# Two more weight slots from a 1 KB descriptor space, and the recurrent gate's 1 - a^2 without a reciprocal

## The chip, the cores and the metric

The kernel runs on one core of a Trainium2 chip. The metric is the device time of one execution in microseconds, and the median of the runs counts. The engines named below are PE (TensorE, with PEld for its weight loads), DVE (VectorE), ACT (ScalarE), POOL (GpSimd) and SP (SyncE, which here does little but issue DMAs).

## The reference

Two transformer blocks run one after the other over 256 tokens of width 1024, batch 1, all in fp32. The first is a hybrid layer: sparse latent attention (each query keeps 64 keys by an index score) beside a gated recurrence. The second has two attentions and a mixture of 32 experts, of which each token takes two. The change touches the recurrence:

```python
r = sigmoid(xb @ w_a + b_a);  i = sigmoid(xb @ w_x + b_x)        # 16 blocks of 64 channels
log_a = -8 * r * softplus(-lam)
a = exp(log_a)
b_in = sqrt(-expm1(2 * log_a)) * (i * x)
h_t = a_t * h_(t-1) + b_in_t                                      # scan over 256 tokens
```

and the way in which all weights, those of the experts above all, come in:

```python
(silu(xb @ w_g[e]) * (xb @ w_u[e])) @ w_d[e]                      # 32 experts, 1024 -> 256 -> 1024
```

## The kernel before

**Weights.** They are one flat DRAM array, cut into pieces, most of them [128, 2048] fp32, that is 1 MB or 8 KB per partition. `load` issues one DMA per piece from SP's queue, in the order of the list `PIECES`: first the dense layers' pieces of both blocks, then per group q of four experts eight pieces gu{q}_0..7 (gate and up) and four pieces dn{q}_0..3 (down). A piece goes into a slot of 8 KB per partition of the pool `bigp`, which has `NBIG` = 19 of them (L26) and shares them with the large activations. `live` counts slots that activations hold; `piece(name)` lets the loads run ahead by what is left. In the expert stage the pieces rotate through `NBIG - 1 + NMO` = 22 slots, four of which are opened late.

**Dense layers.** For each weight piece `split` (L231 to L243) makes a high part (ACT copy, L241) and the rest (a subtraction, L242, on DVE, and on POOL for every second), and `mm3` (L251, L254) multiplies three times per 128 rows. Between pieces `tick()` takes one step from the list `todo`: the choice of 64 keys, the convolution `rnn_conv` (L590, L592), the gates `rnn_gate` (L596 to L611), the attention of a head pair (`attend`, L364 to L403), the scans `rnn_scan` (L613 to L619).

**The gate.** There are eight channel tiles of 128 channels. For tile m, PE makes the two gate products (pg, L600), ACT the tanh of both (L603), a = exp(...) into la (L605) and tt = tanh(u) with u = -log a (L606). Then 1 - a^2 = 2 tanh(u) / (1 + tanh(u)): DVE adds 1 (L607), takes the reciprocal (L608) and multiplies (L609) into `yy`; L610 makes the gated input `ix`. When all eight are there, one square root over 128x2048 elements on ACT (L616, which needs a table load of ACT before it, and another one after it for the next exp or tanh), eight POOL products (L617) and eight DVE scans (L618, printed as TENSOR_TENSOR_SCAN in the trace and as SCALAR_TENSOR_TENSOR in the written order) follow.

**Attention.** `attend` makes the logits of two heads on PE; DVE adds the mask and takes the extreme (L380), ACT makes the exp (L381), DVE the reciprocal of the sums (L382) and the scaling (L384); PE transposes (pt, L391), ACT copies (L393), PE multiplies with the values.

**Experts.** After the router (`trir`, L1021 to L1023, is a constant triangle and a block of ones that PE uses in L1122 to L1127 to rank tokens) each group of four experts gathers its tokens (px L1183, xe L1185), multiplies by gate and up (`products`, pgu L1219), builds the matrix that spreads its result (`spread`, GW L1202 on DVE, pw L1205 on PE), and runs the down product of the group before it (`outputs`: py L1246 on PE, ys L1249 on DVE, acc L1325 on PE, a quarter of the columns at a time). L1354 adds the residual in the round of group 5. L1367 reads a count of further rounds, `nri`, from SP's queue; the loop behind it runs zero times here.

**Order.** A scheduler that simulates a timeline writes the order of each engine's instructions when the kernel is built. Slots, pools and the length of an operation enter into it, so that the order can change at places that the code of the change doesn't touch.

Of the kernel before, what the change touches and what calls it, by code (L numbers as in the profile page):

```python
# [10 lines left out]
F32R = mybir.dt.float32r  # L11
I32 = mybir.dt.int32
AF = mybir.ActivationFunctionType
ALU = mybir.AluOpType
# [3 lines left out]
P = 128  # L18
T = 256
# [3 lines left out]
TAKEN = -3e38  # L23
SLOT = 32
FILL = -2e38
NBIG, NMO, NS2, SPARE, POOLDIV = 19, 4, 7, 0, 2  # L26
KW = 5
SLOPES = [2.0 ** (-0.5 * (h + 1)) for h in range(16)]

# [48 lines left out]
def tile_two_blocks(ctx: ExitStack, tc: tile.TileContext, w, xT_d, xtk_d, vecs_d, rows_d, consa_d, consb_d, wr_d, lam_d, out_d):  # L78
    nc = tc.nc

    cst = ctx.enter_context(tc.tile_pool(name="cst", bufs=1))
# [11 lines left out]
    def gone(n):  # L93

        live[0] -= n
# [8 lines left out]
    def big3(name, dt=F32, m=8):  # L104
        return big(name, dt).rearrange("p (m t) -> p m t", m=m)

    def s2(name, dt=F32, cols=512):
        return s2p.tile([P, cols], dt, tag="s2", name=name)
# [7 lines left out]
    def pst(name):  # L116
        return psp.tile([P, 512], F32, tag="t", name=name)
# [462 lines left out]
    la = big3("la")  # L580
    yy = big("yy")
    yy3 = yy.rearrange("p (m t) -> p m t", m=8)
# [11 lines left out]
    def rnn_gate(m):  # L594
        xc = xcs[m]
        pg = pst("pg")  # L596
        for g in range(2):
            for r0 in (0, 64):
                r = slice(r0, r0 + 64)
                nc.tensor.matmul(pg[r, g * T:(g + 1) * T], rgv[r, m, g, :], xc[r, :T], start=True, stop=True)  # L600
        rt = s2("rt")
        for g in range(2):
            nc.scalar.activation(rt[:, g * T:(g + 1) * T], pg[:, g * T:(g + 1) * T], AF.Tanh, bias=hb[:, 16 + 8 * g + m:17 + 8 * g + m], scale=0.5)  # L603
        tt = s2("tt")
        nc.scalar.activation(la[:, m, :], rt[:, 0:T], AF.Exp, bias=nsp4[:, m:m + 1], scale=nsp4[:, m:m + 1])  # L605
        nc.scalar.activation(tt[:, 0:T], rt[:, 0:T], AF.Tanh, bias=sp4[:, m:m + 1], scale=sp4[:, m:m + 1])  # L606
        nc.vector.tensor_scalar(tt[:, T:2 * T], tt[:, 0:T], 1.0, None, ALU.add)  # L607
        nc.vector.reciprocal(tt[:, T:2 * T], tt[:, T:2 * T])  # L608
        nc.vector.scalar_tensor_tensor(yy3[:, m, :], tt[:, 0:T], 2.0, tt[:, T:2 * T], ALU.mult, ALU.mult)  # L609
        nc.vector.scalar_tensor_tensor(ix[:, m, :], rt[:, T:2 * T], 1.0, xc[:, :T], ALU.add, ALU.mult)  # L610
        gone(m // 7)  # L611

# [13 lines left out]
    for m in range(8):  # L626
        st = [[L(pick, m)], [L(rnn_gate, m)]]
        if m < 7:
            st[0].append(L(rnn_conv, m + 1))
        if m < 4:  # L630
            st[1].append(L(head_k, m))
        elif m < 6:
            st[1].append(L(head_v, m - 4))
        todo += st
# [103 lines left out]
    for i in range(4):  # L738
        ps = mmp("p_wo")
        dense_fm(ps, f"wo{i}", at(mixh), at(mixl), late=i == 0)  # L740
        for j in range(2):
            m = 2 * i + j
# [4 lines left out]
        for j in range(2):  # L747
            m = 2 * i + j
# [31 lines left out]
    for i in range(4):  # L780
# [4 lines left out]
        for j in range(2):  # L785
            m = 2 * i + j
# [190 lines left out]
    def out2(which, i, j):  # L977
        ps = mmp("p_o" + which)
        o = obo[which]
        dense_fm(ps, f"o{which}{i}", at(o), at(o, 4), 4, 512, T * j)  # L980
        return ps, slice(4 * i + 2 * j, 4 * i + 2 * j + 2)

    tga = big3("tga")
    for i in range(2):
        gate2("g2a", 2 * i, tga)
        gate2("g2a", 2 * i + 1, tga)
        for j in range(2):
            ps, m = out2("a", i, j)
# [11 lines left out]
    for i in range(2):  # L1000
        for j in range(2):
            ps, m = out2("b", i, j)
# [15 lines left out]
    for t in (lg[:, :, 36:44], em[:, :, 32:40], top, gtop):  # L1018
        nc.gpsimd.memset(t, FILL)

    trir = cst.tile([P, 2, P], F32R, name="trir")  # L1021
    nc.gpsimd.tensor_copy(trir[:, 0, :], tri)
    nc.gpsimd.tensor_copy(trir[:, 1, :], ones)  # L1023
    ssx = cst.tile([P, 2, 4], F32, name="ssx")
# [493 lines left out]
```

## Time and profile before

| | |
|---|---|
| median of 3 runs | 723.87 us (723.16 to 725.01) |
| profiled execution, its own time | 725.25 us |
| its span | 723.1 us |
| PE busy | 677.8 us, 94% of the span |
| weight loads of PE | 558.9 us, 77% |
| DVE / ACT / POOL busy | 425.4 / 323.8 / 236.6 us |
| read from HBM | 176.67 MB |

A busy share is an average over a dense part, in which PE is nearly always busy, and an expert part from about 515 us on, in which the DMA queue is also busy without a break. The profile's end of a matmul is modelled, so a "busy" PE may be waiting inside. The count and the busy time of the weight loads (PEld) show better how fast a stretch goes forward. In the views, "idle before, releaser" is the time for which an engine sat idle before an instruction and what ended it.

### The profile page before, as it was taken

The numbers are of one execution on the slowest core, as the hardware profiler recorded it, in microseconds if no ns is written. First come the engines' busy times: TensorE is split into PE (matmuls) and PEld (weight loads), VectorE is DVE, ScalarE is ACT, GpSimd is POOL, SyncE is SP. The second block draws the span as 40 slices with busy tenths as digits, with TensorE's granted clock in tenths as the row PEclk, the third lists the DMA queues.
The fourth block names the chain that finished last, engine by engine and source line by source line (L and its number), as shares of the span: only waits on it lengthen the run. The fifth ranks groups of instructions, "written<-read, shape, count | busy, mean of one in ns | idle before, by whom it ended". The sixth has DMA issues, their size and how long they took to land. (4 is left out here: it accounts for less than half of the span.)

```text
span 723.1 us, 13963 instructions
## 1 busy us (share of the span) xinstructions
PE 677.8 (94%) x5463; PEld 558.9 (77%) x5463; DVE 425.4 (59%) x1043; ACT 323.8 (45%) x714; POOL 236.6 (33%) x194
## 2 busy tenths in 40 slices
PE   8989998979999999999999999999999999989983
PEld 7979887968999999998899989999645544534532
DVE  3977999897654767889645565275533222222224
ACT  6355587766755557656476466554100000001022
POOL 1344343466534656965332333372000000000002
PEclk8999999999999999999999999999999999999997
DMA  8991115324647537451035616587899999999992
GB/s 323 417 418 71 60 46 189 117 82 158 228 161 306 184 131 291 159 181 70 5 140 207 233 60 228 180 337 304 336 420 420 419 421 421 420 419 421 420 408 75
DMA packets 26855, 178.69 MB, mean 247 GB/s; under 512 B 3104, under 2 KB 4000, under 8 KB 6176
## 3 DMA queue, kind: packets, MB, share of 16 engines
q1 hardware_dynamic: 26352, 177.15, 62.8%
q8 instruction: 45, 0.74, 0.4%
q10 hardware_dynamic: 432, 0.59, 0.2%
q14 instruction: 26, 0.21, 0.1%
HBM read 176.67 MB, written 1.05 MB: 246 GB/s over the span
## 5 line engine op out<-in xcount | busy, mean ns | idle before, releaser
L1302 POOL TENSOR_TENSOR xg<-xo,fin 128x256 f32<-128x256 f32 (+1 forms) x10 | 6.0, 634 | 211.9 <-DMA w_dn<-in_w_dram 209.4
L1219 PE MATMUL pgu<-w_gu,xe 128*32 128x512 f32 x512 | 65.1, 598 | 0.4 <-DMA w_gu<-in_w_dram 0.4
L1224 ACT ACTIVATE th<-pgu,ss 128x256 f32<-128x256 f32 x8 | 3.8, 475 | 132.8 <-PE pgu L1219 132.8
L1249 DVE COPY ys<-py 128x256 f32<-128x256 f32 (+1 forms) x33 | 13.7, 416 | 46.9 <-PE py L1246 46.8
L1219 PEld LDWEIGHTS pgu<-w_gu,xe 128*32 128x32 f32 x512 | 14.7, 109 | 27.9 <-issue 24.9
L1183 PEld LDWEIGHTS px<-G,xT 128*128 128x128 f32 x256 | 30.2, 192 | 7.6 <-issue 5.5
L1185 DVE TENSOR_TENSOR xe<-px,vecs 128x256 f32<-128x256 f32 (+1 forms) x34 | 13.8, 409 | 37.3 <-PE px L1183 37.3
L1325 PE MATMUL acc<-ys,gwT 128*128 128x256 f32 x112 | 30.6, 405 | 3.5 <-DVE ys L1249 3.5
L1183 PE MATMUL px<-G,xT 128*128 128x128 f32 x256 | 31.9, 278 | 1.4 <-DVE G L1171 0.9
L251 PE MATMUL p_qkv<-hl,hh 128*128 128x256 f32 x192 | 33.2, 294 | 0.0
L381 ACT ACTIVATE lg<-lg,mx 128x128 f32<-128x128 f32 x64 | 28.3, 445 | 8.9 <-DVE mx L380 8.9
L1325 PEld LDWEIGHTS acc<-ys,gwT 128*128 128x128 f32 x112 | 19.6, 190 | 14.6 <-DVE ys L1249 6.6
L251 PEld LDWEIGHTS p_qkv<-hl,hh 128*128 128x128 f32 x192 | 27.7, 198 | 0.3 <-issue 0.2
L1225 DVE SCALAR_TENSOR_TENSOR th<-th,pgu 128x256 f32<-128x256 f32 x8 | 3.4, 421 | 36.8 <-ACT th L1224 36.8
L384 DVE TENSOR_SCALAR lg<-lg,sm 128x128 f32<-128x128 f32 x64 | 21.3, 376 | 0.9
L254 PE MATMUL p_qkv<-hl,hl__3332 128*128 128x256 f32 x96 | 20.3, 293 | 0.0
L391 PE MATMUL pt<-consa,lg 128*128 128x128 f32 x96 | 14.7, 279 | 4.4 <-DVE lg L384 4.4
L242 POOL TENSOR_TENSOR hl<-w_mr,hl 128x512 fp32r<-128x512 f32 x8 | 10.9, 1374 | 20.5 <-ACT hl L241 20.5
L242 POOL TENSOR_TENSOR hl<-w_g2a,hl 128x512 fp32r<-128x512 f32 x8 | 10.4, 1302 | 22.0 <-ACT hl L241 17.8
L251 PE MATMUL p_gr<-xh,hl 128*128 128x256 f32 x64 | 17.6, 302 | 0.0
L251 PE MATMUL p_w<-hl,m2h 128*128 128x256 f32 x96 | 16.2, 284 | 1.2 <-ACT m2h L359 1.2
L592 DVE SCALAR_TENSOR_TENSOR xc<-xr,vecs,xc 128x256 f32<-128x256 f32 x24 | 17.2, 715 | 0.1
(550 smaller groups left out, 2308.9 us busy)
## 6 DMA issues: line engine op xcount, KB each, us to landing
w_gu<-in_w_dram SPq DMA_DIRECT2D x64, 1024.0 KB, 19.8
w_dn<-in_w_dram SPq DMA_DIRECT2D x31, 1024.0 KB, 19.8
w_xr<-in_w_dram SPq DMA_DIRECT2D x4, 1024.0 KB, 11.2
w_q<-in_w_dram SPq DMA_DIRECT2D x4, 1024.0 KB, 17.0
w_mr<-in_w_dram SPq DMA_DIRECT2D x4, 1024.0 KB, 19.8
w_ma<-in_w_dram SPq DMA_DIRECT2D x4, 1024.0 KB, 5.1
w_gr<-in_w_dram SPq DMA_DIRECT2D x4, 1024.0 KB, 4.8
w_rp<-in_w_dram SPq DMA_DIRECT2D x4, 1024.0 KB, 5.1
```

The source lines that it names most:

```text
L242: e.tensor_tensor(l, view, h.bitcast(F32), ALU.subtract)
L251: nc.tensor.matmul(out, l_(k), r_(k), start=first and i == 0, stop=last and i == n - 1)
L254: nc.tensor.matmul(out, al(k), bh(k), start=first and i == 0, stop=last and i == n - 1)
L381: nc.scalar.activation(lg[:, c0:c1], lg[:, c0:c1], AF.Exp, bias=mx[:, b:b + 1], scale=-1.0, accum_out=sm[:, b:b + 1])
L384: nc.vector.tensor_scalar(lg[:, c0:c1], lg[:, c0:c1], sm[:, b:b + 1], None, ALU.mult)
L391: nc.tensor.transpose(pt[:, i * P:(i + 1) * P], pr[hd][:, i * P:(i + 1) * P], ident)
L592: nc.vector.scalar_tensor_tensor(xc[:, :T], xr[:, kk:kk + T], vec(V_CW, kk * 8 + m), xc[:, :T], ALU.mult, ALU.add)
L1183: nc.tensor.matmul(px[:, j * P:(j + 1) * P], x2[:, k, b, :], G[:, b], start=b == 0, stop=b == 1)
L1185: nc.vector.tensor_tensor(xg[k // 4][:, k % 4:k % 4 + n, :], v3(px, n, P), gain2(k, n), ALU.mult)
L1219: nc.tensor.matmul(pgu[32 * j:32 * j + 32, :], xg[k // 4][:, k % 4, 32 * j:32 * j + 32], wgu[:, 512 * j:512 * j + 512], start=k == 0, stop ...
L1249: nc.vector.tensor_copy(ys[:, :n], py[:, :n])
L1325: nc.tensor.matmul(acc[0][:, b, c // 512, c % 512:c % 512 + n], lhsT, rhs, start=q == 0 and c % 512 == 0, stop=q == 6 and c % 512 == T)
```

## The change

There are four edits. (1) `NBIG` goes from 19 to 21: two more slots of 8 KB per partition, and so 24 instead of 22 in the expert stage's rotation. (2) In the gate, 1 - a^2 is made as tanh(u) (1 + a^2): one product of la with itself, and one operation that adds 1 and multiplies by tanh(u); the addition and the reciprocal go. (3) `trir` has no place of its own among the constants any longer but takes one of the seven rotating 2 KB slots `s2`. (4) The program's dynamic DMA scratch size (a space for descriptors that is set aside in SBUF) is set to 1024 bytes.

```diff
--- before.py
+++ after.py
@@ -23,7 +23,7 @@
 TAKEN = -3e38
 SLOT = 32
 FILL = -2e38
-NBIG, NMO, NS2, SPARE, POOLDIV = 19, 4, 7, 0, 2
+NBIG, NMO, NS2, SPARE, POOLDIV = 21, 4, 7, 0, 2
 KW = 5
 SLOPES = [2.0 ** (-0.5 * (h + 1)) for h in range(16)]
 
@@ -604,9 +604,9 @@
         tt = s2("tt")
         nc.scalar.activation(la[:, m, :], rt[:, 0:T], AF.Exp, bias=nsp4[:, m:m + 1], scale=nsp4[:, m:m + 1])
         nc.scalar.activation(tt[:, 0:T], rt[:, 0:T], AF.Tanh, bias=sp4[:, m:m + 1], scale=sp4[:, m:m + 1])
-        nc.vector.tensor_scalar(tt[:, T:2 * T], tt[:, 0:T], 1.0, None, ALU.add)
-        nc.vector.reciprocal(tt[:, T:2 * T], tt[:, T:2 * T])
-        nc.vector.scalar_tensor_tensor(yy3[:, m, :], tt[:, 0:T], 2.0, tt[:, T:2 * T], ALU.mult, ALU.mult)
+
+        nc.vector.tensor_tensor(tt[:, T:2 * T], la[:, m, :], la[:, m, :], ALU.mult)
+        nc.vector.scalar_tensor_tensor(yy3[:, m, :], tt[:, T:2 * T], 1.0, tt[:, 0:T], ALU.add, ALU.mult)
         nc.vector.scalar_tensor_tensor(ix[:, m, :], rt[:, T:2 * T], 1.0, xc[:, :T], ALU.add, ALU.mult)
         gone(m // 7)
 
@@ -1018,7 +1018,7 @@
     for t in (lg[:, :, 36:44], em[:, :, 32:40], top, gtop):
         nc.gpsimd.memset(t, FILL)
 
-    trir = cst.tile([P, 2, P], F32R, name="trir")
+    trir = s2("trir", F32R, 2 * P).rearrange("p (b c) -> p b c", b=2)
     nc.gpsimd.tensor_copy(trir[:, 0, :], tri)
     nc.gpsimd.tensor_copy(trir[:, 1, :], ones)
     ssx = cst.tile([P, 2, 4], F32, name="ssx")
@@ -1504,7 +1504,7 @@
     from concourse import mybir as _mybir
     from concourse.bass_utils import run_bass_kernel_spmd as _run
 
-    nc = _bacc.Bacc("TRN2", target_bir_lowering=False, num_devices=1)
+    nc = _bacc.Bacc("TRN2", target_bir_lowering=False, num_devices=1, dynamic_dma_scratch_size=1024)
     arrays, args = {}, []
     for name, a in _pack(inputs):
         a = np.ascontiguousarray(a)
```

The written order moves at three places that matter for what follows. The first is ACT, around the square root of the gates. A name such as `w_gr_1260` is the 1 MB piece that is being split, `tma` a merge gate's tanh, `lg` the logits of a head. Before:

```order
L606 ACTIVATE tt<-rt,sp_427 128x256
L241 ACTIVATE hl<-w_gr_1260 128x512 x3
L678 ACTIVATE tma<-g,hb 128x256 x2
L381 ACTIVATE lg,sm<-lg,mx 128x128
L241 ACTIVATE hl<-w_gr_1260 128x512
L381 ACTIVATE lg,sm<-lg,mx 128x256
L616 ACT_TABLE_LOAD
L616 ACTIVATE yy<-yy 128x2048
L241 ACTIVATE hl<-w_gr_1471 128x512
L381 ACT_TABLE_LOAD
L381 ACTIVATE lg,sm<-lg,mx 128x128
```

and ACT at the same place of the changed program:

```order
L606 ACTIVATE tt<-rt,sp_431 128x256
L241 ACTIVATE hl<-w_gr_855 128x512
L616 ACT_TABLE_LOAD
L616 ACTIVATE yy<-yy 128x2048
L241 ACTIVATE hl<-w_gr_855 128x512
L678 ACT_TABLE_LOAD
L678 ACTIVATE tma<-g,hb 128x256 x2
L381 ACTIVATE lg,sm<-lg,mx 128x128
L241 ACTIVATE hl<-w_gr_855 128x512
L381 ACTIVATE lg,sm<-lg,mx 128x256
```

The root stood between the exps of the first head pair, with a table load on either side; now it stands ahead of all of them, behind the last gate and one weight copy. On DVE the scans that hang on the root stand behind the first pair's logits in both programs, but three of them now stand together ahead of the pair's softmax sums. Before:

```order
L382 RECIPROCAL sm<-sm 128x2
L384 TENSOR_SCALAR lg<-lg,sm 128x128
L384 TENSOR_SCALAR lg<-lg,sm 128x256
L380 ISA lg,mx<-ps_s,dm 128x128
L380 ISA mx 128x1
L380 ISA lg,mx<-ps_s,dm 128x256
L380 ISA mx 128x1
L242 TENSOR_TENSOR hl<-w_gr_1471,hl 128x512
L618 SCALAR_TENSOR_TENSOR ix<-la,yy 128x256
```

and DVE in the changed program:

```order
L380 ISA lg,mx<-ps_s,dm 128x256
L380 ISA mx 128x1
L618 SCALAR_TENSOR_TENSOR ix<-la,yy 128x256 x3
L242 TENSOR_TENSOR hl<-w_gr_855,hl 128x512
L382 RECIPROCAL sm<-sm 128x2
L380 ISA lg,mx<-ps_s,dm 128x128
L380 ISA mx 128x1
L380 ISA lg,mx<-ps_s,dm 128x256
L380 ISA mx 128x1
L618 SCALAR_TENSOR_TENSOR ix<-la,yy 128x256
L384 TENSOR_SCALAR lg<-lg,sm 128x128
```

Before, the first head's sums and scaling (L382, L384) stood ahead of the first scan; now they stand behind three of them. The second place is SP's queue where the router's count `nri` is read. Before:

```order
L130 DMA w_dn_0_6210<-in_w_dram 128x2048
L130 DMA w_gu_1_6359<-in_w_dram 128x2048
L130 DMA w_dn_3_6355<-in_w_dram 128x2048
L130 DMA w_dn_1_6351<-in_w_dram 128x2048
L130 DMA w_dn_2_6353<-in_w_dram 128x2048
L130 DMA w_gu_0_6357<-in_w_dram 128x2048
L1367 TENSOR_LOAD nri
L1367 ISA x2
```

and SP in the changed program:

```order
L130 DMA w_dn_0_6061<-in_w_dram 128x2048
L130 DMA w_dn_1_6142<-in_w_dram 128x2048
L130 DMA w_dn_2_6206<-in_w_dram 128x2048
L130 DMA w_gu_3_6355<-in_w_dram 128x2048
L130 DMA w_gu_1_6351<-in_w_dram 128x2048
L130 DMA w_dn_3_6347<-in_w_dram 128x2048
L130 DMA w_gu_0_6349<-in_w_dram 128x2048
L130 DMA w_gu_2_6353<-in_w_dram 128x2048
L1367 TENSOR_LOAD nri
L1367 ISA x2
```

Two more loads stand ahead of the read. The third place is PE in the expert stage, at the outputs of the fourth group (`py` its down products, `acc` the sum over groups, `pw` the spread matrix of the next group). Before:

```order
L1219 MATMUL pgu<-w_gu_7_6419,xe 32x512 x4
L1205 MATMUL pw<-consa,GW 128x128 x2
L1246 MATMUL py<-w_dn_0_6421,hT__7104 32x256 x8
L1325 MATMUL acc<-ys,gwT 128x256 x2
L1246 MATMUL py<-w_dn_1_6423,hT__7104 32x256 x8
L1246 MATMUL py<-w_dn_2_6425,hT__7104 32x256 x8
L1325 MATMUL acc<-ys,gwT 128x256 x2
L1246 MATMUL py<-w_dn_3_6427,hT__7104 32x256 x8
L1325 MATMUL acc<-ys,gwT 128x256 x4
L1354 MATMUL acc<-xT,consa 128x512 x4
```

and PE at the same place of the changed program:

```order
L1219 MATMUL pgu<-w_gu_7_6411,xe 32x512 x4
L1205 MATMUL pw<-consa,GW 128x128
L1246 MATMUL py<-w_dn_0_6413,hT__7096 32x256 x8
L1205 MATMUL pw<-consa,GW 128x128
L1246 MATMUL py<-w_dn_1_6415,hT__7096 32x256 x8
L1325 MATMUL acc<-ys,gwT 128x256 x4
L1246 MATMUL py<-w_dn_2_6417,hT__7096 32x256 x8
L1325 MATMUL acc<-ys,gwT 128x256 x2
L1246 MATMUL py<-w_dn_3_6419,hT__7096 32x256 x8
L1325 MATMUL acc<-ys,gwT 128x256 x2
L1354 MATMUL acc<-xT,consa 128x512 x4
```

A down product now stands between the two spread products, and the sums follow two down products instead of one. The two casts of `trir` on POOL moved from the program's start to behind the last weight split.

## Rows read from the trace of the kernel before

**Rows 1.** The page's parts on span and busy time (share, instructions).

```profile
span 723.1 us, 13963 instructions
PE 677.8 (94%) x5463; PEld 558.9 (77%) x5463; DVE 425.4 (59%) x1043; ACT 323.8 (45%) x714; POOL 236.6 (33%) x194
```

**Rows 2.** Windows: PE, PEld, DVE, ACT, POOL busy; granted clock; DMA share; GB/s.

```profile
96.00:108.00 12.00, 11.39 (x95) 10.29 (x91) 11.93 (x17) 9.97 (x22) 5.74 (x5) 1.00 0.17 53
108.00:120.00 12.00, 10.79 (x80) 9.08 (x79) 11.97 (x16) 10.16 (x22) 5.28 (x5) 1.00 0.60 213
120.00:132.00 12.00, 10.98 (x85) 9.16 (x85) 11.89 (x18) 7.91 (x17) 3.77 (x3) 1.00 0.50 177
144.00:156.00 12.00, 9.84 (x72) 7.91 (x70) 11.65 (x19) 7.82 (x22) 11.38 (x10) 1.00 0.00 0
156.00:168.00 12.00, 9.74 (x69) 8.70 (x67) 10.22 (x28) 8.06 (x21) 5.46 (x4) 0.86 0.72 260
180.00:192.00 12.00, 12.00 (x102) 11.09 (x101) 8.96 (x30) 8.86 (x24) 8.14 (x5) 1.00 0.75 264
```

**Rows 3.** PE's waits, 84 to 168 us: total, times, longest.

```profile
PE pt L391 <- DVE lg L384: 4.4, 4, 2.3
```

**Rows 4.** DVE by line, 84 to 144 us: busy, mean ns, idle before.

```profile
L608 DVE RECIPROCAL tt<-tt 128x256 f32<-128x256 f32 x8 | 14.0, 1751 | 0.2
L607 DVE TENSOR_SCALAR tt<-tt 128x256 f32<-128x256 f32 x8 | 2.8, 346 | 0.7 <-ACT tt L606 0.7
L609 DVE SCALAR_TENSOR_TENSOR yy<-tt 128x256 f32<-128x256 f32 x8 | 4.4, 552 | 0.0
L526 DVE TENSOR_TENSOR dm<-wk,consb 128x256 f32<-128x256 f32 x1 | 0.4, 415 | 0.0
```

**Rows 5.** The gate's tiles: ns min/median/max, first and last start.

```profile
L608 DVE RECIPROCAL tt<-tt x8: 1740/1754/1756, 88.6 to 135.2; 128x256 f32<-128x256 f32 x8
L609 DVE SCALAR_TENSOR_TENSOR yy<-tt x8: 411/414/1520, 90.8 to 138.6; 128x256 f32<-128x256 f32 x8
```

**Rows 6.** Timelines of ACT, POOL and DVE at the root: start, us.

```profile
139.90 1.28 ACT L616 ACT_TABLE_LOAD   x1
141.19 1.91 ACT L616 ACTIVATE yy<-yy 128x2048 f32<-128x2048 f32 x1
143.65 1.28 ACT L381 ACT_TABLE_LOAD   x1
...
143.18 7.26 POOL L617 TENSOR_TENSOR yy<-yy,ix 128x256 f32<-128x256 f32 x8 [2.40 <-ACT yy L616]
...
144.40 1.22 DVE L618 TENSOR_TENSOR_SCAN ix<-la,yy 128x256 f32<-128x256 f32 x1
```

**Rows 7.** SP's waits over the span, and the page's row of its queue.

```profile
SPq L130 <- DVE hl L242: 306.6, 46, 24.4
...
q1 hardware_dynamic: 26352, 177.15, 62.8%
```

**Rows 8.** Windows of the expert stage, columns as in Rows 2.

```profile
528.00:612.00 84.00, 79.92 (x678) 41.46 (x674) 23.88 (x76) 4.29 (x10) 0.00 (x0) 1.00 1.01 420
612.00:696.00 84.00, 76.92 (x594) 38.87 (x594) 20.62 (x67) 3.55 (x8) 0.00 (x0) 0.96 1.01 420
```

**Rows 9.** PE's waits, 600 to 712 us.

```profile
PE pgu L1219 <- DMA w_gu<-in_w_dram: 0.4, 1, 0.4
```

**Rows 10.** PE's timeline at the outputs of two groups: start, us.

```profile
609.08 0.33 PE L1205 MATMUL pw<-consa,GW 128*128 128x128 f32 x1
610.42 0.33 PE L1205 MATMUL pw<-consa,GW 128*128 128x128 f32 x1 [1.01 <-DVE GW L1202]
...
620.74 0.59 PE L1354 MATMUL acc<-xT,consa 128*128 128x512 f32 x1
...
665.32 0.33 PE L1205 MATMUL pw<-consa,GW 128*128 128x128 f32 x1
...
675.20 1.05 PE L1183 MATMUL px<-G,xT 128*128 128x128 f32 x8
```

**Rows 11.** The tile trir: its casts and its first use.

```profile
L1022 POOL CAST trir<-consa x1: 297/297/297, 16.5 to 16.5; 128x128 fp32r<-128x128 f32 x1
L1122 PE MATMUL p_pos<-r_A,trir x1: 283/283/283, 514.2 to 514.2; 128*128 128x32 f32 x1
```

## The prediction

> **What bounds the kernel now.** I read the page's span and busy times first, then windows of 12 us, then the waits of PE, and from there the timelines of single places. PE is busy for 94% of the span [rows 1], so a gain has to be found where PE does not advance at its best. The profile models the ends of matmuls, so I take the weight loads as the measure of progress. From 180 to 192 us PE is fed without a gap: 12.00 us busy, 11.09 us of weight loads, DVE busy for 8.96 us [rows 2]. Two stretches fall short of that.
>
> The first is the stretch of the gates, 96 to 132 us. DVE is full there (11.93, 11.97 and 11.89 of 12 us), and the weight loads are at 10.29, 9.08 and 9.16 [rows 2], which is 0.80, 2.01 and 1.93 less than 11.09, together 4.74 us. In time of a fed stretch that is 4.74 x 12 / 11.09 = 5.1 us. By PE's own idle time (12.00 less 11.39, 10.79 and 10.98) it is only 2.8 us.
>
> The second is the attention with the scans, 144 to 168 us: 7.91 and 8.70 us of weight loads, short by 3.18 and 2.39, which is 5.57 x 12 / 11.09 = 6.0 us; by PE's idle time 4.4 us [rows 2]. PE's waits say what ends there last: the softmax's scaling on DVE, 4.4 us in four waits [rows 3].
>
> From 528 to 696 us the DMA engines are busy without a break (1.01) at 420 GB/s, PE is busy for 79.92 and 76.92 of 84 us [rows 8], and it waits for a weight once, for 0.4 us [rows 9]. So weights and PE run nearly level, and neither alone bounds the expert stage. In the dense part the loads wait for slots: 306.6 us of SP's waits are for a split to be done with an old piece [rows 7].
>
> **The gate, on DVE.** Per channel tile an addition and a reciprocal go: 2.8 + 14.0 = 16.8 us in all [rows 4]. One product of two SBUF inputs comes, eight times. The nearest rows are a product of the same shape (415 ns, one sample) and L609, which stands beside it, has the same shape and two SBUF inputs, and took 552 ns on average [rows 4]. I take the latter: 8 x 0.552 = 4.4 us, a saving of 16.8 - 4.4 = 12.4 us of DVE. The ends are L609's shortest and longest, 0.411 and 1.520 us [rows 5]: a saving of 13.5 or of 4.6 us. The changed L609 has the same two inputs as before and an addition for a constant multiplication; I leave its time as it is.
>
> The eight gates lie between 88.6 and 138.6 us [rows 5], so 36 of these 50 us hold 5.75 of them, and DVE is relieved of 5.75 x 1.55 = 8.9 us in 96 to 132: from 35.8 to 26.9 us of 36, or 75%. That is the share at which PE was fed without a gap from 180 to 192 us (8.96 of 12). So the deficit there should go. Between the two measures of it, 2.8 and 5.1 us, I take the middle, 4.0 us. The least it can bring is nothing, if PE was held there by ACT's copies instead (9.97 and 10.16 of 12 us busy [rows 2]).
>
> The row on L609 says that an operation that takes 0.41 us mostly takes up to 1.52 at times, while the reciprocal always took 1740 to 1756 ns [rows 5]. The Trainium skill has a rule for this, on the page "SBUF — State Buffer", section "Who interferes with whom": a VectorE instruction with two SBUF inputs and a GpSimd instruction that reads SBUF shut each other out for a whole instruction, while one with a single SBUF input does not contend. It speaks against this edit, for the reciprocal is of the free kind and the new product of the other. The trace agrees in that L609 stretches and L608 doesn't. By that rule each new product can wait for one POOL split, the saving shrinks towards 4.6 us, and the first rival below gets its mechanism.
>
> **The root.** In the written order the root now stands ahead of the exps of the first head pair and no longer between them. Before, a table load (1.28), the root (1.91) and a table load back (1.28) [rows 6] stood between the pair's exps, and the scaling that PE waits for is behind those. The root comes earlier because the last gate is ready earlier: at 1.55 us per gate, and as DVE is full in front of it, by several microseconds. I take it that the 1.28 + 1.91 = 3.2 us that stood in the pair's way are gained by PE; the second table load still stands ahead of the exps. The bounds are 0 (the order on DVE takes it back, see the third rival) and the whole 6.0 us.
>
> Dense part together: 4.0 + 3.2 = 7.2 us, between 0 and 5.1 + 6.0 = 11.1.
>
> **The slots.** Each dense load waits for a slot, and two more slots let each load go when the load two places ahead went before; the written order of SP has exactly two more loads ahead of the read of the router's count. A piece of 1.05 MB at 420 GB/s [rows 8] takes 2.5 us, so from the router on the weights are 5.0 us ahead, beside what the dense part gains. But PE waits for weights only 0.4 us now [rows 9]; with PE and weights moved by the same 7.2 us, the two slots are worth that 0.4 us, and 4.6 us of lead are left for a faster PE. The lower bound is 0, the upper one the whole 5.0 (the second rival). Behind the read of the count nothing is queued later than before.
>
> **The order in the expert stage.** At the outputs of the fourth group PE took from 609.08 to 620.74 = 11.7 us up to the residual, with 1.01 us of wait for the spread matrix between two pw; at the sixth group, whose order is already pw, a down product, pw, a down product, it took from 665.32 to 675.20 = 9.9 us [rows 10]. The fourth group now has that order: 1.8 us less, between 0 and 1.8. What is late next there is the copy of a down product, which the order of the sixth group has as well. Weights allow it, by the 4.6 us of lead.
>
> **trir and the descriptor space.** The two casts took 0.3 us each [rows 11] and stood where nobody waited for them; they now stand on POOL behind the last split, and the use is at 514.2 us. Even if both were in the way they would cost 0.6 us; I count nothing, for POOL has no other work between them and the use. The slot that trir takes is one of seven, of which the router's stretch needs few. The loads all go through a hardware_dynamic queue [rows 7], and I count the small descriptor space at nothing; the fourth rival is about that.
>
> **Sum.** 7.2 + 0.4 + 1.8 = 9.4 us, off the profiled execution's 725.25 gives 715.85 us. That execution lies 1.38 us above the median of the runs, 723.87, so I forecast 714.5 us. Its own range is 711 to 718.
>
> **Rivals.**
> First, the relief is hidden. PE's idle time in the gates' stretch is only 2.8 us, ACT is busy for 10 of 12 us there, and the new products may stretch under POOL's splits so that DVE stays near full. Then the dense part brings about 1.0 us, and with 2.2 us of the expert stage the time is 725.25 - 3.2 - 1.38 = 720.7 us. For it: POOL is busy 5.74 and 5.28 of 12 us in these windows [rows 2]. Against it: even the saving of 4.6 us takes DVE off its limit.
>
> Second, the weights pace the expert stage, and PE's other waits there (for copies) only fill time that it would have spent on weights. Then the 5.0 us count in full, in place of the 2.2, and the time is 725.25 - 7.2 - 5.0 - 1.38 = 711.7 us. For it: the DMA engines are at 1.01 for 168 us. Against it: a single wait of 0.4 us.
>
> Third, on the other side: the three scans that now stand ahead of the first pair's sums on DVE hold up the softmax. They wait for the root. From the last gate on it is 1.28 + 1.91 us to the end of the root, 7.26 / 8 = 0.91 us to the first POOL product, then three scans of 1.22 us [rows 6], 7.8 us in all, while PE waits for the scaling behind them. If none of it is covered by dense pieces, the root's 3.2 us are not gained either, and the gates bring nothing: 725.25 - 2.2 + 7.8 - 1.38 = 729.5 us; with half of the gates' 4.0 it is 727.5, which I take for its time. It makes the kernel slower from the point at which the stall on PE is longer than what the gates gain and the 2.2 us of the expert stage. For it: PE already waits 4.4 us for this scaling [rows 3]. Against it: the root itself comes earlier than the pair's logits need it, and PE has dense pieces between the pair's steps.
>
> Fourth, the change doesn't do what it says: if the small descriptor space made each load wait for the one before it, the 8 x 12 = 96 expert pieces that now take 2.5 us each in a stream would take, say, twice that, and the time would be some 240 us longer. Against it: the kind of the queue [rows 7]. By the Trainium skill, "DMA: Bandwidth & Descriptors", section "SWDGE vs HWDGE vs iDMA", descriptors of DMAs that SP issues are made in hardware; only those issued from GpSimd need room in SBUF. No row here shows that room.
>
> **Chances.** The forecast has 62%, the first rival 18, the second 9, the third 6, the fourth 1, and 4 are left for no change at all, if what one stage gains is given back in another. A difference of 0.3%, 2.2 us, is what can be told from none. Faster: 62 + 18 + 9, less 2 for that part of the first rival that lies within the bound: 87%. Within it: 4 + 2 = 6%. Slower: 6 + 1 = 7%. The range goes from 710 us (the dense part's full 11.1 us with 2.2 us, 710.6, and a little of the second rival's) to 721 us (the first rival); outside are the third, the fourth, no change, and the second rival with a full dense gain.
>
> **What would show it.** L608 gone from DVE, and the new line's mean near 0.55 us, not 1.5. DVE busy at about 75% in the gates' windows, and weight loads near 11 us in 12. The root's table load ahead of every L381 exp, and PE's waits for L384 under 2 us. PE reaching the router 7 us earlier. SP's loads two pieces ahead, with no wait of PE for a weight, and the fourth group's outputs in under 10 us. The prediction is wrong if PE is fed no better from 96 to 168 us, or if the gain of the dense part comes back as waits for weights in the last groups.

## The result and the profile after

The changed kernel took 714.63 us (median of 4 runs, 714.19 to 716.63), the kernel before 724.17 in the same series; the medians lie 9.5 us apart, and the ratio is 0.9877 (95% interval 0.9856 to 0.9898), that is 8.9 us less (7.4 to 10.4). The forecast was 714.5. That its time came out is luck: of its four terms only the first was about right, the others were off by 1.6 to 4.6 us, in both directions, and the errors cancelled. The traces and the runs below show that.

The profiled execution of the changed kernel took 716.63 us, 8.62 less than the one before. The page's parts on span and busy time, which answer to [rows 1]:

```profile
span 714.6 us, 13950 instructions
PE 674.7 (94%) x5463; PEld 558.4 (78%) x5463; DVE 416.8 (58%) x1035; ACT 324.5 (45%) x714; POOL 237.9 (33%) x194
```

DVE has eight instructions less and 8.6 us less to do. DVE by line, 84 to 144 us, to be held against [rows 4] (L608 is now the product, not the reciprocal):

```profile
L608 DVE TENSOR_TENSOR tt<-la 128x256 f32<-128x256 f32 x8 | 4.9, 615 | 0.1
L609 DVE SCALAR_TENSOR_TENSOR yy<-tt 128x256 f32<-128x256 f32 x8 | 3.4, 425 | 0.9 <-ACT tt L606 0.2
```

Windows of the changed kernel at the gates and at the first softmax (stretch; PE, PEld, DVE, ACT, POOL busy; granted clock, DMA share, GB/s), to be held against [rows 2]:

```profile
96.00:108.00 12.00, 12.00 (x96) 10.51 (x95) 11.64 (x19) 11.11 (x25) 5.97 (x5) 1.00 0.05 13
108.00:120.00 12.00, 12.00 (x93) 10.47 (x91) 10.69 (x17) 10.91 (x24) 5.48 (x5) 1.00 0.77 280
120.00:132.00 12.00, 12.00 (x100) 11.10 (x97) 8.92 (x22) 10.07 (x18) 4.16 (x3) 1.00 0.63 236
138.00:144.00 6.00, 3.62 (x23) 2.54 (x21) 6.00 (x13) 2.42 (x7) 6.00 (x6) 1.00 0.01 1
144.00:150.00 6.00, 5.38 (x20) 4.28 (x21) 5.45 (x18) 3.92 (x10) 1.64 (x2) 0.54 0.11 30
150.00:156.00 6.00, 6.00 (x39) 4.87 (x39) 1.93 (x7) 2.10 (x4) 1.20 (x2) 0.89 0.81 320
```

PE no longer idles in the gates' windows, and the weight loads there fall short of 11.09 by 0.58, 0.62 and nothing, 1.2 us in place of 4.74. DVE did not fall to the predicted 75% there but to 87% (31.25 of 36 us), and PE was fed all the same. From 138 us on there is again a hole: PE idle for 2.4 us while DVE and POOL are full, and behind it a granted clock of 0.54 and 0.89, that is, PE for part of these stretches at the lower of its two levels. PE's waits, 84 to 168 us, to be held against [rows 3]:

```profile
PE ps_s L373 <- DVE mx L380: 1.6, 1, 1.6
PE pt L391 <- DVE lg L384: 1.4, 2, 1.2
```

The root went where the written order put it. ACT, POOL and DVE of the changed kernel there (start, us), to be held against [rows 6]:

```profile
129.64 1.28 ACT L616 ACT_TABLE_LOAD   x1
130.94 1.92 ACT L616 ACTIVATE yy<-yy 128x2048 f32<-128x2048 f32 x1
133.39 1.28 ACT L678 ACT_TABLE_LOAD   x1
135.50 0.39 ACT L381 ACTIVATE lg<-lg,mx 128x128 f32<-128x128 f32 x1
...
132.93 7.66 POOL L617 TENSOR_TENSOR yy<-yy,ix 128x256 f32<-128x256 f32 x8 [4.62 <-ACT yy L616]
...
133.70 3.37 DVE L618 TENSOR_TENSOR_SCAN ix<-la,yy 128x256 f32<-128x256 f32 x3 [1.59 <-POOL yy L617]
139.30 1.44 DVE L384 TENSOR_SCALAR lg<-lg,sm 128x128 f32<-128x128 f32 x2
140.74 3.29 DVE L618 TENSOR_TENSOR_SCAN ix<-la,yy 128x256 f32<-128x256 f32 x2
```

The first pair's logits had been ready on DVE since 132 us. Their exps start at 135.5, behind the root and two table loads, their scaling at 139.3, behind four scans (three stand ahead of the sums, a fourth between sums and scaling), and the next pair's logits (L380) behind two more scans of 1.65 us each. The wait moved earlier in the kernel; it did not go.

In the expert stage, PE of the changed kernel at the outputs of the fourth and the sixth group and at the last gate-and-up piece (start, us), to be held against [rows 10]:

```profile
605.79 0.33 PE L1205 MATMUL pw<-consa,GW 128*128 128x128 f32 x1
...
615.58 0.59 PE L1354 MATMUL acc<-xT,consa 128*128 128x512 f32 x1
...
658.34 0.33 PE L1205 MATMUL pw<-consa,GW 128*128 128x128 f32 x1
...
666.59 3.73 PE L1183 MATMUL px<-G,xT 128*128 128x128 f32 x32
...
679.57 1.06 PE L1219 MATMUL pgu<-w_gu,xe 128*32 128x512 f32 x8 [0.79 <-DMA w_gu<-in_w_dram]
```

The way of PE from one trace to the other can be read off: at the router it is 3.3 us ahead (the tile of `trir`, below), at the residual 620.74 - 615.58 = 5.2, at the end of the sixth group's outputs 675.20 - 666.59 = 8.6, and there it stays. So in this pair of executions 3.3 us came from the dense part and 5.3 from the expert stage; the prediction had 7.2 and 2.2.

The first use of `trir` in the changed kernel, then in a second profile of the same kernel, to be held against [rows 11]:

```profile
L1122 PE MATMUL p_pos<-r_A,trir x1: 283/283/283, 510.9 to 510.9; 128*128 128x32 f32 x1
```

```profile
L1122 PE MATMUL p_pos<-r_A,trir x1: 283/283/283, 508.3 to 508.3; 128*128 128x32 f32 x1
```

The same program reached the router 2.6 us earlier in another execution. This is the scatter against which terms read from one trace have to be held. (From the router on, the second profile is as far ahead of before as the first: its span is 711.9 us, 11.2 less, of which 5.9 stand at the router.)

### The profile page after: what moved, and what is told of

Same layout as the page of the kernel before. It is cut to its first block, busy times and chain, and to the rows that moved or that the text cites. A ratio compares the mean times of both kernels' runs of the same rounds, so it can differ in the third digit from the quotient of the medians.

```text
span 714.6 us, 13950 instructions
## 1 busy us (share of the span) xinstructions
PE 674.7 (94%) x5463; PEld 558.4 (78%) x5463; DVE 416.8 (58%) x1035; ACT 324.5 (45%) x714; POOL 237.9 (33%) x194
## 5 line engine op out<-in xcount | busy, mean ns | idle before, releaser
L384 DVE TENSOR_SCALAR lg<-lg,sm 128x128 f32<-128x128 f32 x64 | 21.2, 374 | 0.8
L242 POOL TENSOR_TENSOR hl<-w_g2a,hl 128x512 fp32r<-128x512 f32 x8 | 10.4, 1303 | 22.0 <-ACT hl L241 22.0
L251 PE MATMUL p_gr<-xl,hl 128*128 128x256 f32 x64 | 17.3, 297 | 0.0
L242 POOL TENSOR_TENSOR hl<-w_rp,hl 128x512 fp32r<-128x512 f32 x8 | 12.0, 1500 | 15.5 <-ACT hl L241 15.5
L242 POOL TENSOR_TENSOR hl<-w_q,hl 128x512 fp32r<-128x512 f32 x8 | 11.4, 1420 | 16.9 <-ACT hl L241 16.8
## 6 DMA issues: line engine op xcount, KB each, us to landing
w_xr<-in_w_dram SPq DMA_DIRECT2D x4, 1024.0 KB, 11.2
```

The costliest lines, as they stand in the source:

```text
L242: e.tensor_tensor(l, view, h.bitcast(F32), ALU.subtract)
L251: nc.tensor.matmul(out, l_(k), r_(k), start=first and i == 0, stop=last and i == n - 1)
L384: nc.vector.tensor_scalar(lg[:, c0:c1], lg[:, c0:c1], sm[:, b:b + 1], None, ALU.mult)
```

## The experiments

**The new gate alone.** The three lines of the gate, in the kernel before.

```diff
-        nc.vector.tensor_scalar(tt[:, T:2 * T], tt[:, 0:T], 1.0, None, ALU.add)
-        nc.vector.reciprocal(tt[:, T:2 * T], tt[:, T:2 * T])
-        nc.vector.scalar_tensor_tensor(yy3[:, m, :], tt[:, 0:T], 2.0, tt[:, T:2 * T], ALU.mult, ALU.mult)
+        nc.vector.tensor_tensor(tt[:, T:2 * T], la[:, m, :], la[:, m, :], ALU.mult)
+        nc.vector.scalar_tensor_tensor(yy3[:, m, :], tt[:, T:2 * T], 1.0, tt[:, 0:T], ALU.add, ALU.mult)
```

> The new gate alone: 19 slots, the old place of trir and the old descriptor space. Its written order is that of the changed kernel in the dense part and that of the kernel before in the expert part. Theory A (the sum of the prediction: the dense part brings 7.2 us, slots and the expert part's order 2.2): 724.2 - 7.2 = 717.0 us. Theory B (the dense part brings only what PE's times in the two traces show, 2.9 to 3.3 us up to the router, and the rest of the 9.5 us comes from the two slots): 720.9 to 721.3 us. The two stand 4 us apart.

Measured: 722.04 us, 0.996 of before (0.9942 to 0.9978), 2.9 us less (1.6 to 4.2). Theory A is out; B's 720.9 to 721.3 us lies within the interval. PE in this run's last group (start, us):

```profile
678.07 1.07 PE L1219 MATMUL pgu<-w_gu,xe 128*32 128x512 f32 x8 [0.68 <-DMA w_gu<-in_w_dram]
...
680.56 1.06 PE L1219 MATMUL pgu<-w_gu,xe 128*32 128x512 f32 x8 [1.43 <-DMA w_gu<-in_w_dram]
...
683.05 1.07 PE L1219 MATMUL pgu<-w_gu,xe 128*32 128x512 f32 x8 [0.80 <-DMA w_gu<-in_w_dram]
...
685.55 1.06 PE L1219 MATMUL pgu<-w_gu,xe 128*32 128x512 f32 x8 [0.80 <-DMA w_gu<-in_w_dram]
```

The last four pieces are used 2.49 us apart, which is the pace of the loads, not that of PE (1.06 us a piece and the matmul that keeps it busy between). PE waits 3.7 us for weights here. This execution also lost time just behind its router, where before, the changed kernel and the run with the descriptor space alone (below) have a granted clock of 1.00 (columns as in the windows above):

```profile
510.00:516.00 6.00, 5.43 (x32) 3.47 (x35) 2.63 (x15) 0.00 (x0) 0.00 (x0) 0.72 0.39 164
```

From the first use of `trir` to the end of the first gate-and-up piece it took 5.4 us, where before and the changed kernel took 3.8.

**The slots alone.** The changed kernel with the old gate put back (the diff above, reversed).

> Two more slots, trir in a rotating slot and the small descriptor space, with the old gate. Its written order is that of the kernel before in the dense part and that of the changed kernel at the outputs of the fourth and the sixth group. Theory A (weights have a lead, the slots are worth 0.4 us and the order 1.8): 724.2 - 2.2 = 722.0 us. Theory B (weights and PE run level to the last group, so that nearly the whole two pieces of 2.5 us count, and the written order lets PE use them): 724.2 - 5 = 719 us, at least 718.5.

Measured: 717.52 us, 0.9902 (0.9879 to 0.9926), 7.1 us less (5.4 to 8.8). Theory A is out; B's 5 us lies just under the interval. In its trace the slots' part is what B says. PE at the last gate-and-up piece:

```profile
680.72 1.06 PE L1219 MATMUL pgu<-w_gu,xe 128*32 128x512 f32 x8 [0.78 <-DMA w_gu<-in_w_dram]
```

It stands 168.6 us behind that run's router (512.1), as in the changed kernel (679.57 - 510.9 = 168.7). With 19 slots it is 173.8 (688.04 - 514.2, before), 173.3 (the descriptor space alone, below) and 175.9 (685.55 - 509.6, the gate alone, of which 1.6 are the lower clock behind its router). From it to the end of the span it is 35 us in all of them (34.9 to 35.4). So the traces give the slots about 5 us (4.6 to 5.7). The timed runs give more, 7.1 here, and 6.0 or 7.1 between the gate alone and the two measurements of the changed kernel. What they show beyond 5 us I can't settle.

**Two more loads.** Into slots of the ring that nobody reads.

```diff
-        i = emitted[0] - len(DENSE)
+        i = emitted[0] - len(DENSE) + more[0]
...
+            if n in ("gu5_0", "gu5_4"):
+                load(n, alloc("w_more"))
+                more[0] += 1
```

> The changed kernel with two more 1 MB loads in the stream, ahead of the first and the fifth gate-and-up piece of the sixth group, into slots of the ring that nobody reads. All weights behind them come 5.0 us later. The dense part's order is untouched; at the outputs of the sixth group the two last down products are parted again, which cost 0.5 us at most in the prediction's rows. Theory A (4.6 us of lead are left): 714.6 + 0.4 + 0.5 = 715.5 us. Theory B (no lead is left in the last group): 714.6 + 5.0 = 719.6 us, 719 if PE still had half a microsecond of its own.

Measured: 719.33 us, 0.9936 (0.9913 to 0.9959), against 0.9877 and 0.9862 for the changed kernel: 4.3 to 5.4 us more. There is no lead. PE's waits in this run, 600 to 712 us (total, times, longest):

```profile
PE pgu L1223 <- DMA w_gu<-in_w_dram: 3.7, 4, 1.4
```

At the sixth group the parted down products cost PE more than the 0.5 us allowed for (10.09 us to the next px, against 8.25 in the changed kernel). But the last four pieces are again 2.49 us apart and PE waits for each of them, so the weights set the end, not this.

**The small descriptor space and trir alone.** The two edits in the kernel before, with 19 slots and the old gate.

```diff
-    trir = cst.tile([P, 2, P], F32R, name="trir")
+    trir = s2("trir", F32R, 2 * P).rearrange("p (b c) -> p b c", b=2)
...
-    nc = _bacc.Bacc("TRN2", target_bir_lowering=False, num_devices=1)
+    nc = _bacc.Bacc("TRN2", target_bir_lowering=False, num_devices=1, dynamic_dma_scratch_size=1024)
```

> The kernel before with the small descriptor space and trir in a rotating slot, but 19 slots and the old gate. PE's written order is that of before word for word. All theories of the prediction but the fourth rival: no change, within 0.3% of before. The fourth rival (a small descriptor space holds up the loads) would show tens of microseconds.

Measured: 723.95 us, 0.9984 (0.9964 to 1.0003): no difference that can be told. PE's order is that of before, so its trace is a second look at the kernel before, and it shows what the first had hidden. PE's waits in this run, 600 to 712 us:

```profile
PE pgu L1219 <- DMA w_gu<-in_w_dram: 2.9, 3, 1.3
```

That is 2.9 us where [rows 9] have 0.4. The reason is in the clock. The kernel before, then this run, at the outputs of the fourth group (columns as in the windows above):

```profile
612.00:618.00 6.00, 5.71 (x44) 2.90 (x48) 1.09 (x3) 0.00 (x0) 0.00 (x0) 0.72 1.02 425
```

```profile
606.00:612.00 6.00, 4.44 (x39) 1.67 (x32) 1.44 (x4) 0.86 (x2) 0.00 (x0) 1.00 1.02 423
612.00:618.00 6.00, 6.00 (x62) 3.61 (x61) 1.68 (x5) 0.00 (x0) 0.00 (x0) 1.00 1.01 422
```

and PE of this run there, with the same order of instructions as in [rows 10]:

```profile
608.20 0.33 PE L1205 MATMUL pw<-consa,GW 128*128 128x128 f32 x1
...
618.24 2.31 PE L1354 MATMUL acc<-xT,consa 128*128 128x512 f32 x5
```

The piece that took 11.66 us in the profiled execution of before takes 10.04 here. The run with the gate alone, with the same order there and a clock of 1.00, also takes 10.04. In the profiled execution of before PE had lost 1.6 us to a clock of 0.72 after the wait of 1.0 us for the spread matrix, which both executions have, and as much again in the fifth group (14.72 against 13.06 us from its pw to the next px, at a clock of 0.84 and 0.88); it came late to the last group, and so found its weights there.

**The changed kernel once more**, as a measure for the rest.

> The changed kernel once more, as the measure for the two runs with a later attention: 0.9877 of before as already measured, within 0.3%.

Measured: 715.33 us, 0.9862 (0.9838 to 0.9886), within 0.2% of the first time.

**The root left out.** The line of L616 is gone; what is computed is not the recurrence.

> The changed kernel with the square root over all eight gates left out, so that 1 - a^2 stands where its root should; the table loads beside it go too, and the scans no longer wait for all eight gates. Theory A (the root is out of the head pair's way already, as the prediction counted it): 713.6 to 714.6 us. Theory C (the root, its products and the scans still hold up the first softmax: 3.0 us of PE's waits between 138 and 145 us, and then a granted clock of 0.54 and 0.89 in the two stretches of 6 us behind them, 2.8 + 0.7 us): up to 6 us less, 708.5 to 711 us.

Measured: 712.91 us, 0.9843 (0.9811 to 0.9874): neither theory. PE's waits, 84 to 168 us:

```profile
PE pg L600 <- DVE xc L592: 1.5, 2, 1.2
PE p_mr L254 <- DVE hl L242: 1.0, 1, 1.0
PE p_uv L251 <- ACT kTs L540: 0.2, 1, 0.2
```

The wait for the softmax is gone, as C has it, but the written order now places the scans among the gates (the first starts at 90.6 us), and PE waits there again as in the kernel before. The run doesn't price the root by itself.

**The attention later**, by two and by three steps.

```diff
-    st = pairs([attn1(m) for m in range(8)])
+    st = [[], []] + pairs([attn1(m) for m in range(8)])
```

> The changed kernel with every step of the first block's attention two steps (one dense piece) later, while the root, its products and the scans stay where they were. Theory C (the root and the scans still hold up the first softmax, which costs PE 3.0 us of waits between 138 and 145 us and up to 3.5 us by the lower granted clock behind them): PE has dense pieces while the root goes, both are gone, and weights and PE both gain: 3 to 6 us less than the changed kernel, a ratio to before of 0.980 to 0.984. Theory D (attention is short of DVE and ACT as a whole, and a wait at its start only moves to a later pair, or to the steps at its end that no dense piece covers): the same as the changed kernel within 0.3%, or up to 3 us more.

> As with the attention two steps later, but three steps. Theory C: no more gain than with two, 0.980 to 0.984 of before, since the wait is gone already. Theory D: each further step only adds to what is uncovered at the end: 0 to 4 us more than the changed kernel.

Measured: 719.30 us, 0.9894 (0.986 to 0.9928), and 717.36 us, 0.9886 (0.9862 to 0.991). C's gain did not come. With two steps the six executions run from 714.35 to 720.56 us; the two shortest have a mean granted clock of 0.988 and 0.990, the others 0.974 to 0.983, and the profiled one is among those. PE's waits with two steps, 84 to 168 us:

```profile
PE ps_s L373 <- DVE mx L380: 2.2, 2, 1.3
PE p_gr L254 <- DVE hl L242: 1.1, 1, 1.1
```

There are 3.3 us of waits, now for a weight split and for the second logits, where the changed kernel had 3.0. Both runs also lose 4 us or more at the end of the attention, where no dense piece covers its steps: the last `po` stands at 224.4 and 224.5 us, against 219.5 in the second profile of the changed kernel, though all three reach the end of w_gr within 0.6 us of each other. (In the first profile of the changed kernel both points are 2.4 us later.)

**The scans behind the softmax.** Each scan takes its initial zero from the sums of a head pair.

```diff
+            if zero is not None:
+                nc.vector.tensor_scalar(zero, sm[:, 0:1], 0.0, None, ALU.mult)
...
-        nc.vector.tensor_tensor_scan(ix[:, m, :], la[:, m, :], yy3[:, m, :], 0.0, ALU.mult, ALU.add)
+        nc.vector.tensor_tensor_scan(ix[:, m, :], la[:, m, :], yy3[:, m, :], zeros[m // 3], ALU.mult, ALU.add)
```

> The changed kernel, with each scan made to stand behind a softmax: its initial value is a zero that DVE makes from the sums of head pair 0 (scans 0 to 2), 1 (3 to 5) or 2 (6 and 7). The root and the POOL products stay; three operations of DVE on one column are added. In DVE's written order the first pair's scaling now stands ahead of all scans. Theory C' (DVE's order is what cost the second term: the scans ahead of the softmax, and PE's wait for it with the lower clock behind): PE's waits of 3.0 us between 138 and 145 us shrink to under 1 us, the granted clock stays at 1.00 there, and the time falls by 3 to 6 us, 0.978 to 0.983 of before. Theory D (DVE and ACT are full there whatever the order): PE waits as long for a later pair, or for the scans themselves at the outputs of w_gr; the same as the changed kernel, 0.986, within 0.3%.

Measured: 714.46 us, 0.9863 (0.9839 to 0.9886), as the changed kernel. PE's waits, 84 to 175 us:

```profile
PE pt L393 <- DVE lg L384: 1.8, 2, 0.9
PE po L402 <- ACT pT L395: 1.3, 1, 1.3
```

The order was changed as meant, and the wait of 1.6 us for the next pair's logits is gone. But PE still waits 1.8 us for the scaling (1.4 before the edit), at a granted clock of 0.72 from 138 to 144 us, and a new wait of 1.3 us came at 168 us. That is theory D, not C', which wanted under 1 us and a clock of 1.00. With the scans out of the way it is ACT that holds up DVE: DVE sat idle until ACT, behind the root and its two table loads, came to the next weight copy.

```profile
134.68 1.16 DVE L242 TENSOR_TENSOR hl<-w_gr,hl 128x512 fp32r<-128x512 f32 x1 [4.46 <-ACT hl L241]
```

**The products on DVE**, run twice, and with late scans and late products together.

```diff
-        nc.gpsimd.tensor_tensor(yy3[:, m, :], yy3[:, m, :], ix[:, m, :], ALU.mult)
+        nc.vector.tensor_tensor(yy3[:, m, :], yy3[:, m, :], ix[:, m, :], ALU.mult)
```

> The changed kernel with the eight products behind the root on DVE in place of POOL. In the changed kernel's trace the products took 1.1 us each on POOL and the scans 1.16 us (median) on DVE beside them, where the shortest scan took 0.66. Theory E (the scans are long because POOL works beside them): the scans fall to about 0.66 us, 8 x 0.5 = 4 us of DVE, against 8 x 0.42 = 3.3 us of products that DVE takes over; DVE's load stays the same, the chain from the root to the last scan gets shorter by 2 us or more, and the time falls by 0 to 2 us. Theory F (the scans' length is their own, or that of their waits): DVE has 3.3 us more to do ahead of the softmax, and the time rises by 1 to 3 us.

> The changed kernel with the products on DVE once more, to see whether it is below the changed kernel (0.9877 and 0.9862 of before). Theory E: 0.984 of before again, at most 0.986. If the first time was luck of the granted clock: 0.986 to 0.988.

> Both edits together: the products on DVE, products and scans behind the softmax of head pairs 0, 1 and 2. Theories C' and E: the lowest time of all, 0.976 to 0.982 of before. Theories D and F: not lower than the changed kernel, 0.986 to 0.990.

Measured: 712.93 us, 0.984 (0.9824 to 0.9857); again 715.50 us, 0.9868 (0.9838 to 0.9898); both edits 715.00 us, 0.9861 (0.9843 to 0.9879). None is shown to be below the changed kernel, and the two traces put the first time down to luck of the granted clock. Its profiled execution and that of the second time have the same instructions and the same waits of PE (1.6 us for the scaling and 1.5 for a weight split). Behind the waits, the first and then the second time:

```profile
150.00:156.00 6.00, 6.00 (x53) 5.56 (x53) 4.95 (x11) 4.92 (x14) 3.67 (x3) 1.00 0.18 75
```

```profile
150.00:156.00 6.00, 6.00 (x25) 4.90 (x25) 3.74 (x12) 2.63 (x8) 1.70 (x2) 0.50 0.11 46
```

In the stretch of 6 us ahead of this one it is 1.00 and 0.66. From the last gate product to the router it took 381.2 us the first time and 385.3 the second. The mechanism of E is there, though. The tile `yy` (ns min/median/max) in the first of these runs, then in the run with late scans, where the POOL products have no scan beside them:

```profile
L617 DVE TENSOR_TENSOR yy<-yy,ix x8: 411/412/1516, 132.4 to 135.8; 128x256 f32<-128x256 f32 x8
L618 DVE TENSOR_TENSOR_SCAN ix<-la,yy x8: 658/668/1714, 136.2 to 143.6; 128x256 f32<-128x256 f32 x8
```

```profile
L620 POOL TENSOR_TENSOR yy<-yy,ix x8: 723/735/1182, 131.1 to 136.4; 128x256 f32<-128x256 f32 x8
```

and in the changed kernel, where products and scans run side by side:

```profile
L617 POOL TENSOR_TENSOR yy<-yy,ix x8: 733/1118/1183, 132.9 to 139.9; 128x256 f32<-128x256 f32 x8
L618 DVE TENSOR_TENSOR_SCAN ix<-la,yy x8: 661/1158/1690, 133.7 to 147.2; 128x256 f32<-128x256 f32 x8
```

## Why the prediction was right in its time and wrong in its terms

**The gate's saving on DVE** was right: 16.8 + 4.4 us were there with the old L609 [rows 4], 4.9 + 3.4 now, which is 12.9 us less where 12.4 was predicted. The product's mean of 615 ns lies near the chosen 552; its median is 422 ns, its longest 1511. So the Trainium skill's rule on two-input operations ("SBUF — State Buffer", "Who interferes with whom") did not decide this term; POOL was busy for only 5.97, 5.48 and 4.16 of 12 us in these windows. The trace agrees with the rule where both engines were full, at the scans, with the 1118 and 1158 ns above against 735 and 668 apart. The prediction told the rule short: by the same section of the Trainium skill a VectorE operation with one SBUF input contends with GpSimd as well when it runs in a 2-port mode, which `tensor_scalar` can enter where its operands allow it. In the kernel before L607, a `tensor_scalar` with one SBUF input, took 276 ns at the shortest, 282 in the median and 789 at the longest; whether it ran in that mode no run here shows.

**The gates' 4.0 us on PE** were about right. By the prediction's own measure it is 4.74 - 1.2 = 3.5 us of weight loads, x 12 / 11.09 = 3.8 us. A better measure is PE's way between two points with the same work between them, in several executions. The gates' products (us, first and last start), before and then in the changed kernel:

```profile
L600 PE MATMUL pg<-xc,w_rg x64: 376/376/427, 72.0 to 129.8; 64*64 64x256 f32 x64
```

```profile
L600 PE MATMUL pg<-xc,w_rg x64: 376/376/427, 72.1 to 126.9; 64*64 64x256 f32 x64
```

Up to the last of these products PE has the same matmuls to do in both kernels. With the first product of the `xr` pieces (29.9 and 30.0 us) as the start and the first use of `trir` at the router as the end:

| us | first `xr` product to last gate product | last gate product to router |
|---|---|---|
| old gate: before, the slots alone, the descriptor space alone | 99.9, 99.8, 100.0 | 384.4, 384.1, 383.8 |
| new gate: changed kernel, once more, the gate alone, two more loads | 96.9, 95.8, 96.8, 96.7 | 384.0, 382.5, 384.8, 383.5 |

Up to the last gate product the new gate brings about 3.4 us by the means (2.9 to 4.2).

**The root's 3.2 us** failed. The step was: the root no longer stands in the first pair's way, so what stood there is gained. Behind the last gate product, where the root and the softmax stand, PE gained 0.4 us by the means of the table, less than the scatter of single executions. By the prediction's sum the stretch of the softmax is now short by 3.00 + 1.27 + 0.68 = 4.9 us of weight loads where it was 5.6, a gain of 0.7 in time (1.7 in the second profile). The root, two table loads and four scans stand ahead of the first scaling, which is the third rival's mechanism with a scan more. It took back this term, not the whole gain. The granted clock behind PE's waits took its share with the old gate too (0.73 from 156 to 162 us before); with the new one it differs between executions, 0.54 and 0.89 in the first profile, and in the second 1.00 from 150 to 156 us and ahead of that:

```profile
144.00:150.00 6.00, 5.88 (x29) 4.95 (x29) 5.37 (x13) 3.02 (x8) 1.44 (x1) 0.72 0.33 102
```

The late attention and the late scans show that the written order alone is not the cause: the wait moves on. What exactly limits that stretch stays open. DVE and POOL, both full and long because of each other, are one candidate, but putting the products on DVE brought nothing that is clear of noise. ACT's chain of root, table loads and exps is another, as the run with late scans has it; leaving the root out did not test it cleanly.

**The slots' 0.4 us** failed, and this is the largest error. The step was: PE waits 0.4 us for weights, so weights are level and two slots give a lead. The gate alone, the slots alone and the two more loads show that the last gate-and-up pieces arrive at the pace of the loads, and that what moves this stream by 5 us moves the end by 4 to 7. The second rival, which had 9%, was the mechanism: the slots counted in full. Its time of 711.7 us was too low because it took over the 7.2 us of the dense part, of which about 3.8 came.

**The order's 1.8 us** at the fourth group was mis-sized. With the clock at 1.00, the old order takes 10.04 us and the new one 9.79: 0.25 us. The rest of the row's 11.66 was the clock in that one execution, which the step of the prediction did not look at. At the sixth group, which was not counted, the new order brought 9.88 - 8.25 = 1.6 us. PE waits for the last piece all the same, so these gains can count only because the stream of weights moved as well; no run has the new order without the slots.

**The descriptor space and trir** cost nothing that can be told, as predicted.

So the sum was 4.0 + 3.2 + 0.4 + 1.8, and what the traces support is about 3.4 from the gates, 0.4 from the root's place, and 5 from the two slots with the order that came with them. The timed runs put 2.9 us (1.6 to 4.2) on gates and root together and 6 to 7 on the slots. The dense part was taken too high by about 3.4 us and the expert stage too low by about 3, and that is why the time came out.

## What to carry to other kernels

Where two streams run nearly level, the wait that a trace shows for one is not what that stream costs: look whether the waiting engine was late for another reason, whether the last uses are spaced at the pace of the transfers, and at a second execution. What a stretch costs is safer read as the time between two points with the same work between them, in several executions, than from one window. A term read from two stretches of one execution has to be compared at the same granted clock, or it prices the clock. An operation that leaves the path's head takes its chain along: ask what now stands ahead of the same consumer.

## What the runs showed of the hardware that I had not expected

The granted clock after the same wait differs between executions of the same instructions: 0.72 in 612 to 618 us before, 1.00 in the run with the same PE order, and 1.00 or 0.50 in 150 to 156 us in two executions of the kernel with the products on DVE. The first 30 us also vary: the first product of the `xr` pieces started at 28.0 us with the gate alone and at 30.0 in the changed kernel, with the same work ahead of it, and between 30 and 72 us two executions of the changed kernel differed by another 1.1 us (its first gate product stands at 72.1 and at 71.0 us). Together this is as large as most terms of the prediction.
